# A decoder layer's down projection: the lo part of u by an adding DMA, and two more pairs of k-tiles by seven products

## The chip, the core and the metric

One core of a Trainium2 chip runs the whole layer as one program. A core has five engines that work on their own and wait for each other by semaphores: PE (TensorE, matrix products into PSUM), DVE (VectorE) and ACT (ScalarE) for elementwise work, POOL (GpSimd) and SP (SyncE), which here mostly start transfers. Transfers between HBM and SBUF, the on-chip memory of 128 partitions, run on 16 DMA engines; SP and POOL each have a queue from which they start them. The metric is the device time of one launch in microseconds. One execution was taken by the hardware profiler; its trace is what the profile lines come from.

## The reference

Everything is float32, with a sequence of 256 and a model width of 2048. The layer is a hybrid attention block and then a feed-forward block:

```python
    x = x + _rmsnorm(mixed @ w_out[layer], norm_attn_post[layer])

    h = _rmsnorm(x, norm_mlp_pre[layer])
    u = jnp.square(jax.nn.relu(h @ w_up[layer]))
    x = x + _rmsnorm(u @ w_down[layer], norm_mlp_post[layer])
```

The change touches the last product only, u (256 x 8192) times w_down (8192 x 2048).

## The kernel before

**Hi and lo parts.** PE multiplies in a rounded form of float32 (`F32R`). To keep float32's accuracy the kernel splits each operand into a rounded hi part and the rest, lo, and forms three products: hi by hi, hi by lo and lo by hi (`three`, L928). `split` (L270) makes them: a copy on ACT writes hi (L273), and a subtraction on DVE writes lo = source - hi (L274).

**The down projection.** The output is made in two halves of 1024 columns, c = 0 and 1. Each half sums over 64 k-tiles of 128, taken in 32 pairs, and needs four PSUM banks: two blocks of 128 rows (b) by two of 512 columns (n). A plain k-tile takes 4 x 3 = 12 matmuls of 512 columns, a pair 24. Some pairs are done by a seven-product scheme (Winograd's form of Strassen's) over the 2 x 2 blocks: `seven_products` (L933) does 7 x 3 = 21 matmuls, into the four banks of the output and four more (`md`), which `close` (L947) adds in once per half. `DOWN_SEVEN` (L102) lists these pairs for each half. A pair by seven products needs sums of weight blocks and of u blocks: `seven` (L311) loads the two weight tiles into `ab_down` by two DMAs from POOL's queue (`load_two`, L335), DVE adds them up into `st_down` (L323 to L328), and four weight tiles (11, b, t and u) are split in place of two. `down_sums` (L890) and `down_split` (L896) make the sums of u and split them.

**Weights.** `Weights` (L153) plans the weight tiles in the order of use. Plain tiles are loaded by SP into five buffers `raw` (L174) and split into eight buffers each of `hi` and `lo`. `get(i)` emits loads and splits up to six tiles ahead of the tile that PE uses next, so the split of tile i + 8 waits until PE has done with tile i.

**u.** The transposed u lies in SBUF as 16 tiles `uT`, each with four k-tiles (a group, g). `split_u` (L873) splits one group into `uhi` and `ulo`, of which there are two buffers each. In the loop of L1094 it is called for the next group right behind the first step of the present one (L1122 to L1124), a step being a plain k-tile or a whole pair by seven products. In the tail, the last two groups of the second half, it is called behind the first of four blocks (L1154). In all it is called 32 times; the first, (0, 0), falls in the up projection and uses buffers of the weights.

**Order.** Each engine runs its instructions in the order in which the program emits them. On ACT the passes for u stand among those for the weights; on POOL the loads of `ab_down` are the only work in this stage, so each is issued as soon as the last reader of the buffer, a DVE split, is done. In each product of three, PE reads (uhi, hi), (uhi, lo) and (ulo, hi) in this order, so `ulo` of a group is first read by the third matmul of it.

**The gains.** `load_gain` (L1066) brings part of the last norm's gain into `g_half` at k-tile 38 of the first half (L1127).

## Time and profile before

| what | value |
|---|---|
| time, median of 3 runs | 1056.94 us (1056.8 to 1057.56) |
| time of the profiled execution | 1059.04 us |
| its span, first to last instruction | 1057.3 us |
| granted clock of PE over the span | 0.997 |
| PE busy | 1044.4 us (99%), 4870 matmuls |
| DVE busy | 809.8 us (77%) |
| ACT busy | 618.9 us (59%) |
| POOL busy | 43.3 us (4%) |
| read from HBM | 201.18 MB |

In the profile's lines L263 is line 263 of the kernel, which is often that of a helper: `mm` is L263, `split` is L273 and L274. `y<-hi,ulo` is a matmul that writes y and reads the tiles hi and ulo. Tiles are named without their numbers. A line of a timeline gives the start in us from the span's start, the length, the engine, the line, the operation, what is written and read with its shape, and in brackets the idle time before it with what ended that. A line of a group gives the count, then busy us and the mean ns of one, then the idle time before them. A line of DMA issues gives the queue, the count, the size of one and the median time from issue to landing. The length of a matmul includes its way through the array: they start every 0.227 us and last 0.39. The down projection runs from about 702 us to 1049.

### The profile page before, as it was taken

What the parts mean: (1) busy time and instruction counts of PE and PEld (TensorE: products, weight loads), DVE (VectorE), ACT (ScalarE), POOL (GpSimd) and SP (SyncE); (2) the same over time, 40 slices, a digit from 0 to 9 for tenths busy, and PEclk for the clock granted to TensorE, in tenths of its full rate; (3) what the DMA queues carried; (4) which work ended last, traced back from release to release, by engine and by line L of the source; (5) the groups of instructions that cost most, each with busy time, mean ns of one, the idle gap of its engine ahead of it and who ended that gap; (6) DMA issues with size and microseconds to landing.
All of it is one profiled execution on the core that took longest, in us unless ns stands there. A gap on an engine that the chain in (4) does not pass through costs nothing.

```text
span 1057.3 us, 13388 instructions
## 1 busy us (share of the span) xinstructions
PE 1044.4 (99%) x4870; PEld 869.5 (82%) x4870; DVE 809.8 (77%) x1073; ACT 618.9 (59%) x826; POOL 43.3 (4%) x82
## 2 busy tenths in 40 slices
PE   9999999999999999999999999999999999999996
PEld 6888889888888888888888888788888888888885
DVE  6486536577557679878889798887788888988995
ACT  7664436565555467566665665666565565656561
POOL 0000000000000000010000000000000000000000
PEclk9999999999999999999999999999999999999998
DMA  9885447454457295646656455567556564667732
GB/s 296 314 268 156 142 132 239 140 167 153 140 178 232 76 349 174 208 155 221 200 197 201 160 199 173 177 226 239 170 191 232 186 219 153 217 219 232 267 126 80
DMA packets 74306, 206.26 MB, mean 195 GB/s; under 512 B 6912, under 2 KB 11520, under 8 KB 73856
## 3 DMA queue, kind: packets, MB, share of 16 engines
q1 hardware_dynamic: 64592, 171.47, 49.8%
q0 software_dynamic: 9216, 33.56, 9.0%
q8 instruction: 38, 0.62, 0.2%
q10 hardware_dynamic: 432, 0.37, 0.1%
q14 instruction: 28, 0.23, 0.1%
HBM read 201.18 MB, written 4.19 MB: 194 GB/s over the span
## 4 chain that ended last, share of the span: by engine, by line
PE 91%; DVE 4%; DMA 2%; issue 2%; ACT 1%; POOL 0%; DVEq 0%; POOLq 0%; ACTq 0%
PE y L263 27%; PE acc_u L263 22%; PE acc_o L263 8%; PE acc_k L263 4%; PE acc_v L263 4%; PE acc_q L263 4%; PE md L263 4%; PE m L263 4%; PE acc_ckv L263 2%; PE acc_ukv L263 2%; PE acc_cq L263 2%; PE acc_uq L263 2%; DVE lo L278 2%; PE rt L267 1%; PE sc_b L263 1%
## 5 line engine op out<-in xcount | busy, mean ns | idle before, releaser
L274 DVE TENSOR_TENSOR lo<-raw,hi 128x1024 fp32r<-128x1024 f32 (+3 forms) x223 | 254.3, 1155 | 110.1 <-ACT hi L273 109.7
L273 ACT ACTIVATE hi<-raw 128x1024 fp32r<-128x1024 f32 (+3 forms) x223 | 219.6, 1002 | 118.1 <-PE y L263 47.3
L263 PE MATMUL y<-hi,uhi 128*128 128x512 f32 x406 | 158.5, 390 | 0.0
L263 PE MATMUL y<-hi,ulo 128*128 128x512 f32 x406 | 158.2, 390 | 0.0
L263 PE MATMUL y<-lo,uhi 128*128 128x512 f32 x406 | 158.1, 389 | 0.0
L263 PE MATMUL acc_u<-hi,hT_hi 128*128 128x512 f32 x386 | 153.6, 398 | 1.9 <-DVE c L953 1.9
L263 PE MATMUL acc_u<-hi,hT_lo 128*128 128x512 f32 x386 | 151.0, 391 | 0.4 <-DVE hT_lo L274 0.4
L263 PE MATMUL acc_u<-lo,hT_hi 128*128 128x512 f32 x386 | 150.8, 391 | 0.0
L278 DVE SCALAR_TENSOR_TENSOR lo<-raw,gcol,hi 128x1024 fp32r<-128x1024 f32 x86 | 107.6, 1279 | 12.6 <-ACT hi L277 12.4
L277 ACT ACTIVATE hi<-raw,gcol 128x1024 fp32r<-128x1024 f32 x86 | 97.8, 1151 | 30.6 <-PE acc_u L263 12.0
L263 PEld LDWEIGHTS y<-lo,uhi 128*128 128x128 f32 x406 | 76.3, 188 | 15.8
L263 PEld LDWEIGHTS y<-hi,ulo 128*128 128x128 f32 x406 | 76.2, 188 | 15.8
L263 PEld LDWEIGHTS y<-hi,uhi 128*128 128x128 f32 x406 | 76.3, 188 | 15.5
L263 PEld LDWEIGHTS acc_u<-hi,hT_hi 128*128 128x128 f32 x386 | 72.6, 188 | 16.6 <-DVE c L953 1.9
L263 PEld LDWEIGHTS acc_u<-hi,hT_lo 128*128 128x128 f32 x386 | 72.5, 188 | 16.1 <-DVE hT_lo L274 0.9
L263 PEld LDWEIGHTS acc_u<-lo,hT_hi 128*128 128x128 f32 x386 | 72.6, 188 | 14.0
L263 PE MATMUL acc_o<-hi,mixT_hi 128*128 128x512 f32 x128 | 51.8, 405 | 0.0
L263 PE MATMUL acc_o<-hi,mixT_lo 128*128 128x512 f32 x128 | 50.2, 392 | 0.0
L263 PE MATMUL acc_o<-lo,mixT_hi 128*128 128x512 f32 x128 | 50.0, 391 | 0.0
L273 ACT ACTIVATE hi<-ab 128x512 fp32r<-128x512 f32 (+1 forms) x36 | 30.3, 842 | 26.6 <-PE acc_u L263 20.7
L263 PE MATMUL m<-hi,st 128*128 128x512 f32 x126 | 45.6, 389 | 0.0
L273 ACT ACTIVATE hi<-st_down 128x1024 fp32r<-128x1024 f32 x30 | 31.3, 1053 | 17.5 <-PE y L263 16.5
(301 smaller groups left out, 1914.1 us busy)
## 6 DMA issues: line engine op xcount, KB each, us to landing
raw<-in_w_down SPq DMA_DIRECT2D x98, 512.0 KB, 4.5
raw<-in_w_up SPq DMA_DIRECT2D x86, 512.0 KB, 4.6
raw<-in_w_in SPq DMA_DIRECT2D x55, 512.0 KB, 5.1
ab<-in_w_up POOLq DMA_DIRECT2D x34, 512.0 KB, 4.9
raw<-in_w_out SPq DMA_DIRECT2D x32, 512.0 KB, 4.3
ab_down<-in_w_down POOLq DMA_DIRECT2D x30, 512.0 KB, 6.2
raw<-in_w_in SPq DMA_DIRECT2D x16, 288.0 KB, 2.9
raw<-in_w_ukv SPq DMA_DIRECT2D x8, 512.0 KB, 4.8
```

The costliest lines, as they stand in the source:

```text
L263: nc.tensor.matmul(out, a, b, start=start, stop=stop)
L267: nc.tensor.transpose(out, a, ident)
L273: nc.scalar.activation(hi, src, AF.Copy)
L274: nc.vector.tensor_tensor(out=lo, in0=src, in1=hi.bitcast(F32), op=OP.subtract)
L277: nc.scalar.activation(hi, src, AF.Copy, scale=g)
L278: nc.vector.scalar_tensor_tensor(out=lo, in0=src, scalar=g, in1=hi.bitcast(F32), op0=OP.mult, op1=OP.subtract)
```

## The change

`DOWN_SEVEN` becomes every third pair: 7, 10, ..., 28 in the first half (8 pairs in place of 7) and 3, 6, ..., 27 in the second (9 in place of 8). `split_u` keeps the subtraction on DVE for the first group only. For the other 31 ACT makes hi, then writes -hi into the tile for lo, and a DMA from POOL's queue adds `uT` to it in SBUF. The load of `g_half` is tied to k-tile 36, since 38 is now part of a pair by seven products.

```diff
-DOWN_SEVEN = ((7, 11, 14, 18, 21, 25, 28), (3, 7, 10, 14, 17, 21, 24, 27))
+DOWN_SEVEN = (range(7, 29, 3), range(3, 28, 3))
...
-        split(uh.rearrange("p k s -> p (k s)"), ul.rearrange("p k s -> p (k s)"), uT[g].rearrange("p k s -> p (k s)"))
+        hi, lo, u = [t.rearrange("p k s -> p (k s)") for t in (uh, ul, uT[g])]
+        if (c, g) == (0, 0):
+            split(hi, lo, u)
+        else:
+            nc.scalar.activation(hi, u, AF.Copy)
+            nc.scalar.activation(lo, u, AF.Copy, scale=-1.0)
+            nc.gpsimd.dma_start(out=lo.bitcast(F32), in_=u, accum_op=OP.add)
         return uh, ul
...
-            if (c, what, k) == (0, "k", 38):
+            if (c, what, k) == (0, "k", 36):
```

## The prediction

> **What bounds the kernel now.** I read the head of the page first, then the busy time of each engine in the stretch of the down projection (702 to 1038 us), then the groups of instructions by line in that stretch. Columns of the second row: length; busy us (and instructions) of PE, PE's weight loads, DVE, ACT, POOL; granted clock; DMA share; GB/s. In the third and fourth: count, busy us and mean ns, and after the last bar the idle time of PE before them.

> ```profile
> span 1057.3 us, 13388 instructions
> PE 1044.4 (99%) x4870; PEld 869.5 (82%) x4870; DVE 809.8 (77%) x1073; ACT 618.9 (59%) x826; POOL 43.3 (4%) x82
> ...
> 702.00:1038.00 336.00, 336.00 (x1492) 278.37 (x1491) 290.38 (x324) 199.75 (x221) 16.13 (x30) 1.00 0.60 202
> ...
> L263 PE MATMUL y<-hi,ulo 128*128 128x512 f32 x406 | 158.2, 390 | 0.0
> L263 PE MATMUL md<-hi,uhi 128*128 128x512 f32 x15 | 5.8, 389 | 0.0
> ```

> PE runs from end to end and waits for nobody in the down projection: 336.00 of 336.00 us busy, idle time 0.0, clock 1.00. DVE is at 290.38/336 = 86%, ACT at 59%. So relief on DVE buys nothing by itself; only fewer matmuls can shorten this stage, and every wait that PE gets is new time. What decides is how early `ulo` is there. I took that from the timeline (start, length), one group of four k-tiles after another. Two kinds of groups differ.

> ```profile
> 764.74 0.39 PE L263 MATMUL y<-hi,uhi 128*128 128x512 f32 x1
> 764.71 1.06 ACT L273 ACTIVATE uhi<-uT 128x1024 fp32r<-128x1024 f32 x1 [1.38 <-PE y L263]
> 765.81 1.23 DVE L274 TENSOR_TENSOR ulo<-uT,uhi 128x1024 fp32r<-128x1024 f32 x1 [1.22 <-ACT uhi L273]
> 774.94 0.39 PE L263 MATMUL y<-hi,uhi 128*128 128x512 f32 x1
> 775.39 0.39 PE L263 MATMUL y<-hi,ulo 128*128 128x512 f32 x1
> ...
> 785.82 0.39 PE L263 MATMUL md<-hi,uhi 128*128 128x512 f32 x1
> 786.07 3.10 ACT L273 ACTIVATE hi<-raw 128x1024 fp32r<-128x1024 f32 x3 [1.19 <-issue]
> 789.08 1.05 ACT L273 ACTIVATE uhi<-uT 128x1024 fp32r<-128x1024 f32 x1
> 793.16 1.22 DVE L274 TENSOR_TENSOR ulo<-uT,uhi 128x1024 fp32r<-128x1024 f32 x1
> 796.02 0.39 PE L263 MATMUL y<-hi,uhi 128*128 128x512 f32 x1
> 796.47 0.39 PE L263 MATMUL y<-hi,ulo 128*128 128x512 f32 x1
> ```

> At 764.74 PE begins a group, which frees the other pair of u buffers, and ACT makes the next `uhi` at once; the third matmul of the next group (775.39) is the first that reads `ulo`. In the second kind the group begins with a seven-product pair (`md` at 785.82). The split is emitted only behind all seven products, so three weight passes stand ahead of it on ACT, and `uhi` starts at 789.08, 3.3 us after the group's start. Today `ulo` is still done at 794.38, 2.1 us early.

> **The change, part by part.**

> *Matmuls.* A pair by seven products takes 21 matmuls in place of 24. The lists have 8 + 9 pairs in place of 7 + 8, so 2 x 3 = 6 fewer. The group from 785.82 to 796.02 is 21 + 24 = 45 matmuls in 10.20 us, 0.227 us each: **-1.36 us**, all on PE's path.

> *DVE and ACT.* 31 subtractions leave DVE (the first split keeps the old way), and 31 passes of the same size go to ACT.

> ```profile
> L274 DVE TENSOR_TENSOR ulo<-uT,uhi 128x1024 fp32r<-128x1024 f32 x27 | 33.0, 1220 | 8.1 <-ACT uhi L273 8.1
> L273 ACT ACTIVATE uhi<-uT 128x1024 fp32r<-128x1024 f32 x27 | 28.4, 1052 | 15.8 <-PE y L263 15.8
> L323 DVE TENSOR_TENSOR st_down<-ab_down 128x1024 f32<-128x1024 f32 x15 | 18.3, 1219 | 0.0
> L327 DVE TENSOR_TENSOR st_down<-st_down,ab_down 128x512 f32<-128x512 f32 x15 | 10.4, 693 | 0.5
> L274 DVE TENSOR_TENSOR lo<-ab_down,hi 128x512 fp32r<-128x512 f32 (+1 forms) x30 | 28.1, 952 | 0.4 <-ACT hi L273 0.4
> L274 DVE TENSOR_TENSOR slo<-st_down,shi 128x512 fp32r<-128x512 f32 x15 | 10.3, 685 | 0.0
> L886 DVE TENSOR_TENSOR st_down<-uT 128x256 f32<-128x256 f32 x12 | 5.0, 418 | 0.0
> L887 DVE TENSOR_TENSOR st_down<-st_down,uT 128x128 f32<-128x128 f32 x12 | 3.5, 292 | 0.4
> L273 ACT ACTIVATE hi<-ab_down 128x512 fp32r<-128x512 f32 (+1 forms) x30 | 25.2, 839 | 7.8 <-PE y L263 4.2 <-ACT hi L273 3.6
> L273 ACT ACTIVATE shi<-st_down 128x512 fp32r<-128x512 f32 x15 | 9.4, 626 | 6.0 <-DVE st_down L888 5.9
> ```

> DVE: -31 x 1.22 = -37.8 us. Two more seven-product pairs add two times (1.22 + 2 x 0.69 sums of weights, 0.42 + 2 x 0.29 sums of u, 0.69, and 2 x 0.95 + 2 x 1.22 lo parts, less 2 x 1.22 for the plain tiles) = some 12 us. DVE falls to about 265 of 336 us. ACT: 31 x 1.05 = +32.6, and 2 x (2 x 0.84 + 0.63) = 4.6 for the pairs (the hi passes of their other two weights are those of the plain tiles), to some 237 of 336. Both are hidden behind PE, whose weights are split six tiles ahead; if that cover went, ACT's second pass would cost 1.05 us a group. I book 0.

> *`ulo` by DMA: the term that decides.* ACT makes hi, then -hi, each 1.05 us, then POOL issues the DMA, and PE waits for its landing. Behind POOL's wait for ACT stand the loads of `ab_down`, for which DVE's sums wait; behind PE's wait stands everything. In the first kind of group: 764.71 + 2 x 1.05 + 0.05 for the hand-over (`uhi` ended at 765.77, DVE began at 765.81) = 766.86, needed at 775.39: **8.5 us** for issue to landing. In the second: 789.08 + 2.15 = 791.23, needed at 796.47: **5.25 us**. A group of 48 matmuls has 8.5 + 3 x 0.227 = 9.2 us. The last split comes behind a quarter of its group:

> ```profile
> 1028.38 1.05 ACT L273 ACTIVATE uhi<-uT 128x1024 fp32r<-128x1024 f32 x1
> 1038.56 0.39 PE L1085 MATMUL y<-hi,ulo 128*128 128x512 f32 x1
> ```

> 1038.56 - 1030.53 = 8.0 us. A group begins with a seven-product pair where the pair is even: 10, 16, 22, 28 in the first half and 6, 12, 18, 24 in the second, **8 of 31** (6 before). Of the rest 9 have 8.5 us, 13 have 9.2, one 8.0.

> The trace has no adding DMA, and none from SBUF to SBUF. The nearest rows (KB each, median us from issue to landing; the last is one issue alone, that of 885.8 us; the first gives the share of the 16 engines' span):

> ```profile
> q0 software_dynamic: 9216, 33.56, 9.0%
> ...
> raw<-in_w_down SPq DMA_DIRECT2D x98, 512.0 KB, 4.5
> ab<-in_w_up POOLq DMA_DIRECT2D x34, 512.0 KB, 4.9
> ab_down<-in_w_down POOLq DMA_DIRECT2D x30, 512.0 KB, 6.2
> ...
> uT<-xkeep SPq DMA_DIRECT2D x4, 512.0 KB, 9.3
> out<-uT SPq DMA_DIRECT2D x6, 256.0 KB, 2.5
> ...
> ab_down<-in_w_down POOLq DMA_DIRECT2D x1, 512.0 KB, 4.6
> ```

> One pass of 512 KB keeps the engines 9.0% x 1057.3 / (34 + 30) = 1.5 us each. Lower end: the store from SBUF of 256 KB and half a pass more, 2.5 + 0.75 = 3.25 us, with the add free. Upper end: 9.3 us, four transfers of this size at once on a queue in use. Between them I start from `ab_down`, same queue, size and stage: 6.2; less what a source in SBUF saves (4.5 - 3.25 = 1.25); plus one more pass, since the add has two operands to fetch (1.5): **6.5 us**, an estimate. Against 5.25 that is 1.25 us late, 8 times: **+10.0 us**. Against 8.0 and more it is in time. What is late next is nothing further: a PE that stops leaves weights, ACT and DVE ahead of it.

> [...]

> *The loads of `ab_down`* now stand behind the `ulo` DMA on POOL. Today:

> ```profile
> 757.43 0.54 POOL L337 DMA_DIRECT2D ab_down<-in_w_down  x1 [20.38 <-DVE lo L274]
> 759.70 0.54 POOL L337 DMA_DIRECT2D ab_down<-in_w_down  x1 [1.73 <-DVE lo L274]
> 768.69 1.22 DVE L323 TENSOR_TENSOR st_down<-ab_down 128x1024 f32<-128x1024 f32 x1
> 771.28 1.22 DVE L274 TENSOR_TENSOR lo<-raw,hi 128x1024 fp32r<-128x1024 f32 x1
> ```

> In the changed order they issue at 766.86 + 0.54 = 767.4 and 767.9, land 6.2 later and a pass (1.5) behind the other, at 775.6. DVE's sums then run 775.6 to 778.2 (2.6 us) in place of 768.69, so DVE stands 6.9 us; the next lo is ready at 779.4. PE wants it after 24 matmuls of the group that starts at 774.94, plus one: 780.6. Spare 1.2 us: cost 0, and DVE's freed time pays for the wait.

> *The earlier load of `g_half`* (two DMAs of 256 KB on SP's queue, two k-tiles earlier) lies among loads that run five buffers ahead: 0. The 2 MB that move from SP's queue to POOL's with the pairs: 0.

> **Sum.** -1.36 + 10.0 = +8.6 us. The profiled execution took 1059.04 us, span 1057.3 and 1.7 around it, 2.1 above the median of the runs shown, 1056.94. So 1067.7 for its like, and for the median **1065.6**.

> **Rivals.**

> 1. *The landing stays under 5.25 us* (not slower). For it: 4.6 us in the quiet case, and the 3.25 bound. Against: 6.2 is the median of the same queue in this stage, where the DMA engines are 60% busy. Then only the matmuls count: 1056.9 - 1.4 = 1055.6, that is -0.13%.
> 2. *The landing passes 8.5 us.* For it: 9.3, and a second operand at a time when queues are shared. At 9.3: 8 x 4.05 + 9 x 0.8 + 13 x 0.1 + 1.3 = 42, hence 1098.
> 3. *DVE is held by the late `ab_down`*, and the weights' lo parts come late. It decides where these loads take over 6.2 + 1.2 = 7.4 us. At 9.3 it is 1.9 us behind each of some 7 even pairs, 13 us: 1069 with the `ulo` in time, more with it late. Against it: a PE that has waited for `ulo` widens this margin.
> 4. *More than the matmuls is won.* No row speaks for it; PE has no idle time to give back.

> **How the numbers follow.** Forecast (landing between 5.25 and 8.5 us, 8 groups late) 0.53; rival 1 0.25; rival 2 0.13; rival 3 0.05; rival 4 0.04. A measurement of this kernel can tell about 0.2%, 2.1 us, from no change. Slower by more needs 3.5 us of waits, a landing over 5.7 us: most of the forecast, and rivals 2 and 3: 0.66. Same: rival 1 and the low edge of the forecast: 0.30. Faster: 0.04. The forecast's own range is 1055.6 to 1055.6 + 8 x 3.25 = 1081.6; the range takes in rival 1 at its low end and a first step of rival 2, 1055.0 to 1084.

> **What would show it.** PE idle before `y<-hi,ulo` and `md<-hi,ulo`, put down to the DMA of `ulo`, 8 times at the end of groups that begin with an even pair, and none in the others; the median landing of that DMA, 6.5 by me, under 5.25 by rival 1, over 8.5 by rival 2; idle time of DVE before L323 put down to `ab_down`, some 7 us at even pairs, without PE waiting for a weight's `lo`; 6 fewer matmuls. The forecast is wrong if PE has no idle time in the stage, or if it waits at nearly every group.

## The result, and the profile after

The changed kernel took 1127.88 us (median of 6 runs, 1123.51 to 1130.47) against 1057.63 us of the kernel before on the same chip: ratio 1.0661, 95% interval 1.0639 to 1.0684. That is 70 us slower, where 9 were forecast. The profiled execution has a span of 1125.9 us, 68.6 more than before. Up to 690 us the two traces agree (PE busy 686.9 and 685.3 us), so all of it arises in the down projection.

The head of the page, and the down projection as one stretch (length; busy us and count of PE, its weight loads, DVE, ACT, POOL; granted clock; DMA share; GB/s):

```profile
span 1125.9 us, 13456 instructions
PE 1066.5 (95%) x4864; PEld 879.1 (78%) x4864; DVE 784.7 (70%) x1060; ACT 650.3 (58%) x863; POOL 73.1 (6%) x117
...
702.00:1106.00 404.00, 356.05 (x1477) 287.17 (x1476) 263.66 (x310) 229.54 (x257) 46.00 (x65) 0.95 0.70 208
```

The stretch is 404 us long where it was 336. PE stands for 404.00 - 356.05 = 47.95 us of it, and the clock granted to PE is 0.95 in place of 1.00, which costs about 0.05 x 404 = 20 us more. With the six matmuls less, 47.95 + 20 - 1.4 = 67 of the 68.6 us are accounted for. So there are two losses, and only the first was in the forecast: PE waits, and behind the waits it runs slowly.

Who waited for whom in the stage, of PE, DVE and ACT (us in total, times, longest):

```profile
PE y L263 <- DMA ulo<-uT: 25.4, 8, 6.3
PE md L263 <- DMA ulo<-uT: 13.7, 6, 5.0
PE y L263 <- DMA ulo<-ab: 6.8, 2, 4.0
PE y L263 <- DVE lo L274: 2.0, 2, 1.0
...
DVE st_down L323 <- DMA ab_down<-in_w_down: 114.7, 17, 8.9
...
ACT hi L273 <- DMA ab_down<-in_w_down: 48.4, 20, 6.3
```

The DMA issues of the stage (KB each, median us to landing), and the software queue's packets, MB and share of the 16 engines:

```profile
q0 software_dynamic: 14256, 51.91, 17.3%
...
raw<-in_w_down SPq DMA_DIRECT2D x94, 512.0 KB, 6.3
ab_down<-in_w_down POOLq DMA_DIRECT2D x34, 512.0 KB, 9.5
...
ulo<-uT POOLq DMA_DIRECT2D x27, 512.0 KB, 6.7
```

The adding DMA lands after 6.7 us; the forecast had 6.5. Yet PE waits for it 16 times and not 8. What had changed beside it is `ab_down`: 9.5 us from issue to landing in place of 6.2, and every one of DVE's 17 sums of weights waits for it, where none did before. ACT waits for it too, and that was not in the prediction at all. One turn of the loop, from the timeline:

```profile
739.75 1.82 DVE L274 TENSOR_TENSOR lo<-ab_down,hi 128x512 fp32r<-128x512 f32 x2
...
744.50 0.87 POOL L885 DMA_DIRECT2D ulo<-uT  x1 [8.64 <-ACT ulo L884]
745.06 1.41 POOL L337 DMA_DIRECT2D ab_down<-in_w_down  x2
...
752.36 0.39 PE L263 MATMUL y<-hi,uhi 128*128 128x512 f32 x1
752.42 0.63 ACT L273 ACTIVATE hi<-ab_down 128x512 fp32r<-128x512 f32 x1 [3.52 <-DMA ab_down<-in_w_down]
755.35 1.23 DVE L323 TENSOR_TENSOR st_down<-ab_down 128x1024 f32<-128x1024 f32 x1 [7.64 <-DMA ab_down<-in_w_down]
755.36 1.06 ACT L273 ACTIVATE hi<-ab_down 128x1024 fp32r<-128x1024 f32 x1 [2.30 <-DMA ab_down<-in_w_down]
758.14 1.06 ACT L273 ACTIVATE hi<-st_down 128x1024 fp32r<-128x1024 f32 x1 [1.72 <-DVE st_down L328]
759.11 1.04 ACT L883 ACTIVATE uhi<-uT 128x1024 fp32r<-128x1024 f32 x1
761.40 0.88 POOL L885 DMA_DIRECT2D ulo<-uT  x1 [14.93 <-ACT ulo L884]
761.97 1.38 POOL L337 DMA_DIRECT2D ab_down<-in_w_down  x2
...
768.42 0.79 PE L263 MATMUL md<-hi,ulo 128*128 128x512 f32 x1 [3.25 <-DMA ulo<-uT]
769.01 0.63 PE L263 MATMUL y<-hi,uhi 128*128 128x512 f32 x1
769.44 0.63 PE L263 MATMUL y<-lo,uhi 128*128 128x512 f32 x1
```

Read it from the top. DVE has read `ab_down` for the last time at 741.57 (739.75 + 1.82), and before the change the next load would have been issued at once (there at 759.70, behind a last reader that ended at 759.40). Now POOL first waits for ACT's pass that makes -hi, starts the `ulo` DMA at 744.50, and issues the loads at 745.06, 3.5 us after their buffer came free. The second lands at 755.3, 9.7 us after its issue at 745.6. A new group of PE begins at 752.36, which frees the buffers for the next `uhi`. In the kernel before, ACT made it in that moment in such a group (764.71 and 764.74 in the prediction). But on ACT the hi passes over `ab_down`, and one over the sums that DVE makes of it, stand ahead, each held up, and `uhi` starts at 759.11, 6.8 us behind the group's start. So the `ulo` DMA goes out at 761.40, lands 7.0 us later, and PE, which needs it at 765.2, waits until 768.42. The next loads stand behind this DMA, and their buffer comes free late as well, at about 762, since DVE's work on `ab_down` was late by as much. Each late load delays the `uhi` and the `ulo` behind which the next loads stand. I call this the loop.

The last two rows also show the second loss: the matmuls behind the wait last 0.63 us and start 0.43 apart, about twice the usual 0.227. The next stretch gives the clock there.

```profile
768.40:774.20 5.80, 5.78 (x14) 4.52 (x15) 0.92 (x1) 1.94 (x3) 0.00 (x0) 0.50 0.76 261
774.20:780.00 5.80, 5.80 (x27) 4.79 (x26) 5.73 (x8) 5.01 (x6) 0.88 (x1) 1.00 0.41 82
```

Half the clock for about six microseconds: 14 matmuls where 27 fit.

### The profile page after: what moved, and what is told of

Its sections match the earlier page's. It is cut to its first block, busy times and chain, and to the rows that moved or that the text cites. A ratio compares the mean times of both kernels' runs of the same rounds, so it can differ in the third digit from the quotient of the medians.

```text
span 1125.9 us, 13456 instructions
## 1 busy us (share of the span) xinstructions
PE 1066.5 (95%) x4864; PEld 879.1 (78%) x4864; DVE 784.7 (70%) x1060; ACT 650.3 (58%) x863; POOL 73.1 (6%) x117
## 3 DMA queue, kind: packets, MB, share of 16 engines
q0 software_dynamic: 14256, 51.91, 17.3%
## 4 chain that ended last, share of the span: by engine, by line
PE 76%; issue 14%; DMA 7%; DVE 2%; POOL 1%; ACT 0%; DVEq 0%; POOLq 0%; SPq 0%; ACTq 0%
PE acc_u L263 24%; PE y L263 13%; PE acc_o L263 8%; PE m L263 5%; PE acc_k L263 4%; PE acc_v L263 4%; PE acc_q L263 3%; DMA ulo<-uT 3%; PE acc_ckv L263 2%; PE acc_ukv L263 2%; PE acc_cq L263 2%; DMA ab_down<-in_w_down 2%; PE md L263 2%; PE acc_uq L263 1%; DMA ulo<-ab 1%
## 5 line engine op out<-in xcount | busy, mean ns | idle before, releaser
L274 DVE TENSOR_TENSOR lo<-raw,hi 128x1024 fp32r<-128x1024 f32 (+3 forms) x219 | 248.6, 1153 | 94.5 <-ACT hi L273 93.8
L273 ACT ACTIVATE hi<-raw 128x1024 fp32r<-128x1024 f32 (+3 forms) x219 | 214.5, 999 | 101.3 <-PE y L263 25.0
L263 PE MATMUL y<-hi,ulo 128*128 128x512 f32 x394 | 160.3, 407 | 32.2 <-DMA ulo<-uT 25.4
L263 PE MATMUL y<-lo,uhi 128*128 128x512 f32 x394 | 159.1, 404 | 2.0 <-DVE lo L274 2.0
L263 PE MATMUL y<-hi,uhi 128*128 128x512 f32 x394 | 159.3, 404 | 0.0
L263 PE MATMUL acc_u<-hi,hT_hi 128*128 128x512 f32 x386 | 153.4, 397 | 0.3 <-DVE c L959 0.3
L263 PE MATMUL acc_u<-hi,hT_lo 128*128 128x512 f32 x386 | 150.9, 391 | 0.4 <-DVE hT_lo L274 0.4
L263 PE MATMUL acc_u<-lo,hT_hi 128*128 128x512 f32 x386 | 150.6, 390 | 0.0
L263 PEld LDWEIGHTS y<-hi,ulo 128*128 128x128 f32 x394 | 77.5, 197 | 52.9 <-DMA ulo<-uT 28.8
L277 ACT ACTIVATE hi<-raw,gcol 128x1024 fp32r<-128x1024 f32 x86 | 97.8, 1151 | 28.1 <-PE acc_u L263 12.2
L323 DVE TENSOR_TENSOR st_down<-ab_down 128x1024 f32<-128x1024 f32 x17 | 20.8, 1225 | 114.7 <-DMA ab_down<-in_w_down 114.7
L263 PEld LDWEIGHTS y<-lo,uhi 128*128 128x128 f32 x394 | 77.2, 196 | 19.6 <-DVE lo L274 2.9
L263 PEld LDWEIGHTS y<-hi,uhi 128*128 128x128 f32 x394 | 77.6, 197 | 15.8
L263 PEld LDWEIGHTS acc_u<-hi,hT_lo 128*128 128x128 f32 x386 | 72.5, 188 | 16.0 <-DVE hT_lo L274 0.8
L263 PEld LDWEIGHTS acc_u<-hi,hT_hi 128*128 128x128 f32 x386 | 72.6, 188 | 15.1 <-issue 0.7
L263 PEld LDWEIGHTS acc_u<-lo,hT_hi 128*128 128x128 f32 x386 | 72.6, 188 | 14.2
L273 ACT ACTIVATE hi<-ab_down 128x512 fp32r<-128x512 f32 (+1 forms) x34 | 28.7, 844 | 55.9 <-DMA ab_down<-in_w_down 48.4
L263 PE MATMUL acc_o<-hi,mixT_hi 128*128 128x512 f32 x128 | 51.8, 405 | 0.0
L263 PE MATMUL acc_o<-hi,mixT_lo 128*128 128x512 f32 x128 | 50.2, 392 | 0.0
L263 PE MATMUL acc_o<-lo,mixT_hi 128*128 128x512 f32 x128 | 50.0, 391 | 0.0
L885 POOL DMA_DIRECT2D ulo<-uT x27 | 23.9, 886 | 370.7 <-ACT ulo L884 365.8
## 6 DMA issues: line engine op xcount, KB each, us to landing
raw<-in_w_down SPq DMA_DIRECT2D x94, 512.0 KB, 6.3
raw<-in_w_up SPq DMA_DIRECT2D x86, 512.0 KB, 4.5
raw<-in_w_in SPq DMA_DIRECT2D x55, 512.0 KB, 5.1
ab<-in_w_up POOLq DMA_DIRECT2D x34, 512.0 KB, 4.8
ab_down<-in_w_down POOLq DMA_DIRECT2D x34, 512.0 KB, 9.5
raw<-in_w_out SPq DMA_DIRECT2D x32, 512.0 KB, 4.3
ulo<-uT POOLq DMA_DIRECT2D x27, 512.0 KB, 6.7
```

The source lines that it names most:

```text
L263: nc.tensor.matmul(out, a, b, start=start, stop=stop)
L273: nc.scalar.activation(hi, src, AF.Copy)
L274: nc.vector.tensor_tensor(out=lo, in0=src, in1=hi.bitcast(F32), op=OP.subtract)
L277: nc.scalar.activation(hi, src, AF.Copy, scale=g)
L323: tt(out=two[0], in0=two[1][:, 0:2, :], in1=two[1][:, 1:4:2, :], op=OP.add)
L885: nc.gpsimd.dma_start(out=lo.bitcast(F32), in_=u, accum_op=OP.add)
```

## The experiments

Theory A: the order on POOL, with ACT and DVE behind it, is the larger part; the loads of `ab_down` stand behind the `ulo` DMA and hold up the next `uhi`. Rival B: the adding DMA is by itself too slow for its window. Rival C: the two more pairs by seven products cost the time. All times below are against the kernel before on the same chip in the same runs.

**Each part of the change alone.** First the DMA with the old lists of pairs (and `g_half` back at k-tile 38), then the new lists with the old split.

```diff
-DOWN_SEVEN = (range(7, 29, 3), range(3, 28, 3))
+DOWN_SEVEN = ((7, 11, 14, 18, 21, 25, 28), (3, 7, 10, 14, 17, 21, 24, 27))
```

> The changed kernel with the old lists of pairs (7 and 8 by seven products), so ulo by the adding DMA alone. Theory A (order on POOL: the loads of ab_down stand behind the ulo DMA, land late, and ACT's hi passes that read ab_down stand ahead of the next uhi): the same waits, a few fewer since there are 15 loads in place of 17 and some pairs lie four apart: DVE waits 70 to 110 us for ab_down, PE 25 to 45 us for ulo, time 1090 to 1120. Rival B (the adding DMA is by itself too slow for its window): PE waits at nearly as many groups as with the new lists, ulo landing 6 to 7 us, DVE's waits for ab_down play no part; 1090 to 1125 as well. Rival C (the closer pairs are what costs): no waits, 1057 to 1062.

```diff
-        if (c, g) == (0, 0):
-            split(hi, lo, u)
-        else:
-            nc.scalar.activation(hi, u, AF.Copy)
-            nc.scalar.activation(lo, u, AF.Copy, scale=-1.0)
-            nc.gpsimd.dma_start(out=lo.bitcast(F32), in_=u, accum_op=OP.add)
+        split(hi, lo, u)
```

> The new lists of pairs with the old split (lo by DVE's subtraction everywhere), so the pairs alone. Theories A and B: PE without waits or nearly so, 6 matmuls fewer, -1.4 us: 1056 to 1057; DVE busy some 12 us more in the stage, near 90%. Rival C: DVE is too full, the lo parts of weights come late, over 1070.

The DMA alone: 1116.21 us, ratio 1.0548 (1.0533 to 1.0564). The pairs alone: 1057.36 against 1057.93, ratio 0.9990 (0.9981 to 0.9999). With the pairs alone PE waits for nobody, and DVE keeps up:

```profile
702.00:1038.00 336.00, 336.00 (x1491) 278.22 (x1490) 300.60 (x343) 202.41 (x226) 18.33 (x34) 1.00 0.60 202
...
ab_down<-in_w_down POOLq DMA_DIRECT2D x34, 512.0 KB, 6.1
```

Rival C falls. The DMA carries the loss; but with it the closer pairs do cost, 1127.88 - 1116.21 = 12 us; that they do so by bringing more loads into the loop is likely and not shown. The time of the DMA alone lies in the ranges of both A and B, so it does not tell them apart; DVE's 84.8 us of waits for `ab_down` are what A expected, and `ulo` landed after 5.7 us there. And `ab_down` lands in 6.1 us with the same 34 loads as long as there is no `ulo` DMA.

**The loads of `ab_down` ahead of the `ulo` DMA.** They are emitted two weight tiles earlier.

```diff
+                def early(c=c, k=k):
+                    load_two(dpl["ab"], nc.gpsimd, io["w_down"][2 * k * P:(2 * k + 2) * P, c * CW:(c + 1) * CW])
-                ts, after = plan_seven(*seven_down(c, k), after, ((2, q), (1, parts_q)))
+                ts, after = plan_seven(*seven_down(c, k), after, ((2, early), (2, q), (1, parts_q)))
```

> The changed kernel with the two loads of ab_down of each pair emitted two weight tiles earlier, so that on POOL they mostly stand ahead of the ulo DMA. Theory A: DVE's waits for ab_down fall from 114.7 us to under 30, ACT no longer waits for ab_down, PE waits only in the 8 groups that begin with an even pair, 1 to 2 us each, and the clock dips are fewer: 1064 to 1080. Rival B: PE's waits for ulo stay at 35 us or more, over 1105.

1098.15 us, ratio 1.0366 (1.0335 to 1.0396). From the waits of PE, DVE and ACT:

```profile
PE y L263 <- DMA ulo<-uT: 20.2, 7, 4.2
PE y L263 <- DMA ulo<-ab: 4.7, 2, 2.4
...
DVE st_down L323 <- DMA ab_down<-in_w_down: 56.2, 14, 5.3
...
ACT hi L273 <- DMA ab_down<-in_w_down: 0.5, 1, 0.5
```

ACT's waits for `ab_down` are gone but for 0.5 us, and of PE's 16 waits 9 are left, 8 of them at the end of a group that begins with an even pair. The kind was as expected; the size was not. DVE still waits 56.2 us and not under 30, and the time is 18 us over the range. PE's 8 waits last 2.3 to 4.2 us, not 1 to 2, and all but the ninth (0.9 us) are followed by half clock (the granted clock from 702 to 1038 us is 0.95). In these 8 groups the window is the one of the forecast (5.2 to 5.3 us, once 4.9), but the DMA lands after 7.5 to 9.2 us, while the median of all is 6.8. So 30 of the 70 us came from this order, with the later landings that go with it.

**The window.** The split is emitted ahead of a group's first step, so that no group has less than 8.5 us. First with the loads emitted as in the change, and then together with the earlier loads. In the expectation of the second, "the run before it" is `e3_ab_early`.

```diff
+            nxt = (c, g + 1) if g < GT - 1 else (1, 0)
+            if nxt not in us:
+                us[nxt] = split_u(*nxt)
             if what == "k":
                 w = weights.get(tiles[0])
...
-            nxt = (c, g + 1) if g < GT - 1 else (1, 0)
-            if nxt not in us:
-                us[nxt] = split_u(*nxt)
             if (c, what, k) == (0, "k", 3):
```

> The changed kernel with nothing but the split of u emitted ahead of each group's first step, so that each window is 8.5 us or more, while the loads of ab_down stay behind the ulo DMA. If the short windows of the 8 groups were most of the loss, PE's waits go under 10 us and the time under 1075. If the order on POOL is the larger part (e4_ab_early_u_early, with the loads behind the ulo DMA in about half the pairs, took 1099), DVE's waits for ab_down stay at 85 to 115 us and the lo parts of weights come late in place of ulo: 1090 to 1115.

1154.71 us, ratio 1.0910 (1.0890 to 1.0930), worse than the change itself:

```profile
PE y L263 <- DVE lo L274: 59.4, 12, 12.5
PE y L263 <- DMA ulo<-uT: 3.3, 2, 2.9
...
DVE st_down L323 <- DMA ab_down<-in_w_down: 141.6, 17, 16.2
```

Here `ulo` is nearly always in time, and yet PE loses more. It now waits for the lo parts of weights, since DVE stands 141.6 us for `ab_down`, which comes behind an `ulo` DMA each time. The expectation did not have it this dear. This is not the window alone, though: with the splits emitted earlier, the loads of 7 pairs (13, 19, 25 and 9, 15, 21, 27) now stand behind one more `ulo` DMA on POOL than in the change. Those of pair 13, for one, go out at 774.10, 7.6 us after their buffer came free; in the change it was at once. PE's seven waits of 6 us and more, 57 of the 59.4 us, stand in the groups of exactly these seven pairs. So the run shows the order at work, and not what the window is worth.

> As the run before it, and the split of the next u emitted ahead of a group's first step and not behind it, so that uhi starts when the group starts, also where it begins with a seven-product pair. Theory A: every window is 8.5 us or more, a landing of 6.7 us is in time, PE without waits: 1055 to 1060, at best the 1.4 us of the six matmuls below the kernel before. Rival B: at landings near 9 us PE still waits in many groups: over 1085.

1099.30 us, ratio 1.0387 (1.0372 to 1.0401).

```profile
DVE st_down L323 <- DMA ab_down<-in_w_down: 88.4, 17, 9.1
...
ACT hi L273 <- DMA ab_down<-in_w_down: 42.2, 20, 4.7
```

Theory A missed by 40 us. `e3_ab_early` had put the loads of 10 of the 17 pairs ahead of one `ulo` DMA. With all splits moved forward too, they stand behind it again: the order on POOL is that of the changed kernel, pair for pair. DVE's waits for `ab_down` are 88.4 us against 56.2 in `e3_ab_early`, and ACT's 42.2 against 0.5. So I moved the split only in the groups that begin with a seven-product pair (the same edit under `if what == "w" and nxt not in us`).

> As e3_ab_early (9 waits of PE, 8 of them in the groups that begin with an even pair), and the split emitted ahead of the first step only in these groups. Theory A: their window grows from 5.25 to 8.5 us, the waits of 2.3 to 4.2 us there go to under 1 us, and the clock dips behind them too: 1056 to 1066. Rival B: landings grow to 9 us or more, waits stay: over 1080.

1071.95 us, ratio 1.0128 (1.0111 to 1.0146).

```profile
PE y L263 <- DMA ulo<-uT: 7.5, 4, 4.2
PE y L263 <- DMA ulo<-ab: 0.3, 1, 0.3
...
DVE st_down L323 <- DMA ab_down<-in_w_down: 43.1, 11, 8.6
...
ulo<-uT POOLq DMA_DIRECT2D x27, 512.0 KB, 6.5
```

Two edits of order take 56 of the 70 us away, with the same DMAs and the same arithmetic. That is 6 us over the upper end that I had given: PE still waits four times, where the DMA landed after 8.4 to 10.7 us; 6.5 is only the median. The other 14 us are for the most part these waits (7.8 us) and the half clock behind them.

What an edit did to the order is read from POOL's rows: how many `ulo` DMAs have gone out when the loads of a pair do. The table has it for the first 8 of the 17 pairs; the others go on in the same way.

| run | `ulo` DMAs ahead of the loads of pairs 7, 10, 13, 16, 19, 22, 25, 28 | windows | us |
|---|---|---|---|
| as changed | 2, 4, 5, 7, 8, 10, 11, 13 | 8 short | 1127.9 |
| `e3_ab_early` | 1, 3, 5, 6, 8, 9, 11, 12 | 8 short | 1098.2 |
| `e4_ab_early_u_early` | 2, 4, 5, 7, 8, 10, 11, 13 | long | 1099.3 |
| `e10_ab_early_u_early_at_w` | 1, 3, 5, 6, 8, 9, 11, 12 | long | 1072.0 |
| `e7_u_early` | 2, 4, 6, 7, 9, 10, 12, 13 | long | 1154.7 |

The first four rows form a square. The earlier order is worth 29.7 us with short windows and 27.4 with long ones, the longer windows 28.6 and 26.2: the two losses are of one size and nearly add up. So the order is not the larger part, as theory A had it, but about half, and rival B holds for the short windows.

**The loads on SP's queue.** One word in `seven_down`, `nc.sync` for `nc.gpsimd`, first alone and then with the split ahead of each group's first step.

> The changed kernel with the loads of ab_down issued from SP's queue, among the loads of raw, so that none stands behind a ulo DMA. Theory A: landings of ab_down near those of raw, DVE's waits for ab_down under 40 us in place of 114.7, PE waits left in the 8 groups that begin with an even pair alone, 2 to 3 us each with a clock dip behind most: 1080 to 1100. Rival B (the adding DMA's own slowness, whatever stands behind it): over 1110.

1133.07 us, ratio 1.0704 (1.0672 to 1.0736), a miss:

```profile
PE y L263 <- DMA ulo<-uT: 36.8, 8, 7.5
PE md L263 <- DMA ulo<-uT: 10.8, 5, 2.7
...
DVE st_down L323 <- DMA ab_down<-in_w_down: 1.3, 2, 1.2
...
ab_down<-in_w_down SPq DMA_DIRECT2D x34, 512.0 KB, 5.0
ulo<-uT POOLq DMA_DIRECT2D x27, 512.0 KB, 9.0
```

DVE's waits went from 114.7 to 1.3 us as theory A has it, and still nothing was won: the `ulo` DMA, now beside all the loads of SP's queue, lands after 9.0 us in place of 6.7, and that alone makes it late. In all PE waits 55.9 us for it. This is rival B's mechanism, and B's range, in a setting of its own.

> As e5_ab_from_sp, and each split of u emitted ahead of its group's first step. Theory A: every window 8.5 us or more and nothing late ahead of uhi on ACT: PE's waits for ulo under 5 us, 1055 to 1064. Rival B: the DMA engines are too full for landings under 8.5 us, waits in many groups, over 1080.

1074.06 us, ratio 1.0143 (1.0118 to 1.0168). With longer windows the same queues give landings of 6.7 us again, PE waits 11.8 us for `ulo`, and DVE 7.1 for `ab_down`. That lies between the two expectations. Why the same DMA takes 9.0 us in the one and 6.7 in the other, with only its time of issue moved, shows in the single issues. In the first run 17 of the 31 `ulo` DMAs go out within 4.5 us behind a pair of `ab_down` loads, and 14 of these land after 10.0 to 12.0 us; the other 14 of the 31 land after 4.5 to 9.6. In the second only 3 go out so, and land after 9.6 to 11.6; the other 28 after 4.7 to 9.4. So it falls together with the loads; no run moved this alone.

**The price of the add.** A plain copy in place of the add (`accum_op` left out; ulo then holds u).

> The changed kernel with a plain copy of u in place of the add, same size, queue and order; ulo then holds u and not u - hi, so the output is another. It prices the second operand. If an add costs one more pass, as the prediction had it, the landing of ulo falls from 6.7 us by about 1.5 to near 5.2, and DMA time of the software queue falls from 17.3% to about 13%; PE's waits halve, 1085 to 1110. If only order counts, the landing and the time change little: over 1115.

1098.50 us, ratio 1.0382 (1.0361 to 1.0403).

```profile
q0 software_dynamic: 14256, 51.91, 13.9%
...
ab_down<-in_w_down POOLq DMA_DIRECT2D x34, 512.0 KB, 8.0
...
ulo<-uT POOLq DMA_DIRECT2D x27, 512.0 KB, 4.1
```

The copy lands after 4.1 us, the add after 6.7: 2.6 us and not 1.5 for the second operand, with what it does to the traffic beside it (`ab_down` lands sooner beside the copy, too). The engines' own time is nearer to the guess: 17.3% of 1125.9 us less 13.9% of 1095.1 us (its span) is 42.6 us, 1.37 for each of 31 DMAs. Even at 4.1 us, under every window of the forecast, 40 us are lost: DVE still waits 86.2 us for `ab_down`, which stands behind the copies in the order of the change. That is theory A without the add.

**More pairs with the old split.** Since the pairs alone were the one part that gained, I tried two more of them (9 and 10), some two pairs apart, with the loads emitted earlier.

```diff
+DOWN_SEVEN = ((7, 10, 12, 15, 17, 20, 22, 25, 28), (3, 6, 8, 11, 13, 16, 18, 21, 24, 27))
```

> The old split on DVE, two more pairs by seven products than the changed kernel (9 and 10, some two pairs apart), and the loads of ab_down emitted two weight tiles earlier. 12 matmuls fewer than before, -2.7 us: 1054 to 1056 if DVE keeps up (its work in the stage is about 290 + 25 of 336 us) and the loads land in time; a wait of DVE for ab_down that reaches PE as a late lo of a weight would make it 1060 or more.

1067.67 us, ratio 1.0079 (1.0065 to 1.0093). This time PE waits for DVE: 6.0 us for `ulo` and 1.5 for a `lo`. So there may be a real need behind the change: with the subtraction on DVE, this one longer list already costs more than its matmuls save. The new lists with the old split are the only version tried that is not slower than the kernel before.

## Why the prediction was wrong

The forecast had 10.0 us of waits, in 8 groups. These 8 waited 27.3 us (1.6 to 6.3 each). Another 8 groups, for which it had 0, waited 18.6, and the lo parts of weights cost 2.0. About 20 us of half clock had no term.

- **Matmuls, -1.36 us.** Right in size as far as it can be seen: the pairs alone gave 0.6 us with an interval of 0.1 to 2.0, and their profiled span is 1055.6 against 1057.3.
- **DVE and ACT, 265 and 237 us in the stage.** Right: 263.66 and 229.54. Taking DVE's load away bought nothing, as said.
- **The landing of `ulo`, 6.5 us.** Right as a median, 6.7, and by luck: it was put together with errors that cancel, 2.6 us for the second operand and not 1.5, and a copy inside SBUF at 4.1 and not 6.2 - 1.25 = 4.95. And one median for all places was too little. In `e3_ab_early`, where the 8 windows are as forecast, the 8 DMAs land after 7.5 to 9.2 us and cost 23.9 us of waits, not 10.0.
- **The loads of `ab_down`: "Spare 1.2 us: cost 0".** This is the step that failed. The loads were taken to land 6.2 us after issue and one pass behind the `ulo` DMA, 7.7 in all; they took 9.5, 1.8 more, where 1.2 were to spare. On the path that I followed, a late lo of a weight, this cost PE only 2.0 us. The cost came on another, since I followed the wait on DVE only. The same tiles are read by ACT's hi passes, and on ACT these stand ahead of the next `uhi`: `uhi`, which I took to start when its group starts, started 6.8 us behind that in the turn shown. The windows of 5.25 and 8.5 us were fixed numbers in the forecast, but a late load makes them shorter (the 8 of 5.25 were 1.9 to 5.3), and a later `ulo` DMA makes the next load later. `e3_ab_early` shows the first: with earlier loads ACT's waits for them go from 48.4 to 0.5 us, and PE's 8 waits outside the forecast's groups to one. `e7_u_early` shows what one more `ulo` DMA ahead of the loads costs: 57 us of waits at seven pairs.
- **"What is late next is nothing further: a PE that stops leaves weights, ACT and DVE ahead of it."** Wrong. POOL's queue is not ahead; its loads had waited for nothing but their buffers and now wait for ACT. And PE itself is slower behind a wait: about 20 of the 70 us are half clock, for which the sum had no term.
- **The rivals.** Rival 3 named the mechanism, the loads behind the `ulo` DMA, and gave it 0.05 and 13 us, since it was priced on DVE's path alone, with no way back to `uhi`. Its limit of 7.4 us leaves out the pass that the sum counts behind the `ulo` DMA; with it the limit is 8.9, and 9.5 is beyond both. Rival 2's condition, a median landing of over 8.5 us, did not hold in the changed kernel; two single landings took 9.6 and 9.7. The sign in the profile that I had named, 8 waits at the end of groups with an even pair and none elsewhere, is what `e3_ab_early` shows (with one more of 0.9 us), where ACT no longer waits for the loads.

## What to carry to other kernels

Here an operation moved to an engine that only issued transfers made that engine wait (POOL for ACT, 30 times from 690 us on in the changed kernel, never before the change). For such a move, list every transfer that now stands behind the wait, then every reader of it on every engine, and see whether one of those readers stands ahead of the operation that was moved. Here one did, and windows measured before the change did not hold (8 of 5.25 us became 1.9 to 5.3). After an edit of order, count in the rows what really stands ahead of each transfer: two of the edits here did not give the order that they were meant to give. A wait of PE should be priced with the half clock that may follow it: of the 11 waits of 1.97 us or more in the changed kernel 9 were followed by 3.41 or 6.83 us of it.

## What the runs showed of the hardware

```profile
851.23 0.73 PE L263 MATMUL y<-hi,ulo 128*128 128x512 f32 x1 [2.26 <-DMA ulo<-ab]
847.92:851.33 3.41, 1.15 (x6) 0.65 (x4) 3.34 (x6) 3.00 (x4) 0.70 (x1) 1.00 1.03 284
851.33:854.75 3.42, 3.42 (x9) 2.65 (x10) 1.51 (x2) 0.47 (x1) 0.18 (x1) 0.50 0.93 299
```

```profile
969.62 0.50 PE L263 MATMUL y<-hi,ulo 128*128 128x512 f32 x1 [2.31 <-DMA ulo<-uT]
965.33:968.75 3.42, 1.99 (x9) 1.31 (x7) 3.42 (x4) 2.17 (x3) 0.00 (x0) 1.00 1.04 242
968.75:972.16 3.41, 2.54 (x11) 2.12 (x12) 3.34 (x6) 1.58 (x2) 1.97 (x3) 1.00 1.03 270
```

The first wait lies in one stretch, of which PE was busy for 1.15 us, and the next has clock 0.50. The second is split, 1.44 and 0.87 us, and nothing follows. The 27 waits of over 0.25 us in the two runs all go this way: the 17 with 1.96 us or more in one stretch were followed by half clock, the 10 with 1.88 or less were not.

**The adding DMA landed later than a copy.** Its median was 6.7 us against 4.1 for a copy of the same 512 KB in the same place; the loads beside the copy landed sooner as well, 8.0 against 9.5 us.
